# An encoder step on one Trainium2 core: half of an up projection's feature chunks by Strassen's seven products

## The chip, the core and the metric

The kernel runs on one core of one Trainium2 chip. TensorE (PE) multiplies; its weight loads (PEld) overlap with it. VectorE (DVE), ScalarE (ACT) and GpSimd (POOL) work element by element; SyncE (SP) issues DMAs. The metric is device time in microseconds, the median of several runs. A profiled execution is one run more, taken with the hardware profiler. "hi" and "lo" below are the two parts into which every float32 operand is split; TensorE multiplies in its float32r form, and a product of two operands takes three matmuls: hi x hi, hi x lo and lo x hi.

## The reference, cut to what matters

384 tokens (256 of a prompt, 16 new ones of each of 8 streams) go through one layer. The part that the change touches is the feed-forward block:

```python
h2 = rmsnorm(x, norm_ffn_g)                 # 384 x 2048
up = h2 @ w_up                              # 2048 x 11264
g_half = up[..., :D_FF]                     # D_FF = 5632
u_half = up[..., D_FF:]
ext_f = jnp.concatenate([ffn_buf.astype(g_half.dtype), g_half], axis=1)
gc = causal_dwconv(ext_f, ffn_dw_w, ffn_dw_b)          # 3 taps along the frames
x = x + (jax.nn.silu(gc) * u_half) @ w_down            # 5632 x 2048
new_ffn = ext_f[:, -(FFN_CONV_W - 1):]      # the last two rows of each stream go out as state
```

Ahead of it stand a combined input projection, attention, a convolution branch and an output projection, which the change leaves as they are, but for the last step of the output projection (below).

## The kernel before

**Tiling.** Tokens are three tiles of 128. Features are chunks of 128: 16 of them for the up projection. The 5632 columns of each half are 11 groups of 512; a *panel* is 512 columns. Group g has a gate panel and an up panel, then a convolution along the frames, SiLU, a product, and the activations `act{g}` of 4 chunks, hi and lo. The down projection reads the activations of several groups and adds to `y`, four panels of 512 columns.

**A matmul** takes one chunk of one token tile (128 x 128, loaded as weights) and 512 columns of one weight chunk. A weight tile `raw` has two chunks (512 KB, one DMA on SP's queue, three buffers). ScalarE casts it to `hi` (L149), VectorE subtracts to `lo` (L150), three buffers each. `gemm` asks for the split two tiles ahead (`ahead`), then does the 18 matmuls of the tile (2 chunks, 3 token tiles, 3 matmuls, L251 to L253): this is called a *step* below. An up panel has 8 steps, 144 matmuls. PSUM has 5 banks `acc` and 3 `misc`; a panel holds three.

**Order.** TensorE's order is the program's (`pe_order`). The other engines' order is set by the scheduler from priorities: splits get 150, what leaves PSUM 400, turns 100. `FFN_PLAN` does the up projections of groups 0 to 3, the down projection of 0 to 2, then 4 to 6 and 3 to 5, and so on.

**After a panel** ScalarE moves three banks to token rows `tok`, scaled by the row's norm (L1003). `turn` brings them to feature rows: VectorE transposes 32 x 32 blocks (L274), 16 DMAs on SP's queue move the blocks between partitions (L278, `uT<-tb`). For the gate, ScalarE copies into `extf` (L1012), GpSimd copies the halo frames (L1018, the old state at L1019), VectorE does 12 tap operations (L1027, L1029), ScalarE SiLU. `new_state` takes the last frames through a TensorE transpose (L1036) and two DMAs. For the up half, VectorE multiplies (L1058), ScalarE casts (L1060), VectorE subtracts (L1061).

**Ahead of the block**, after each panel of the output projection `norm_panel` transposes `y` and makes the feature chunks `xg`, hi (L960) and lo (L961); `second_norm` makes the row norms `rs2`.

Of the kernel before, what the change touches and what calls it, by code (L numbers as in the profile page):

```python
# [15 lines left out]
P = 128  # L16
DM = 2048
NT = 384
# [23 lines left out]
def hybrid_step(  # L42
# [27 lines left out]

    def acc_tile():
        return acc.tile([P, 512], F32, tag="acc", name="acc")

    def misc_tile():
        return misc.tile([P, 512], F32, tag="misc", name="misc")

# [51 lines left out]
    def stream_tile():  # L128
        return rp.tile([P, 2, 512], F32, tag="raw", bufs=3, name="raw")
# [44 lines left out]
    FFN_PLAN = [("up", g) for g in range(4)] + [("down", (0, 1, 2))]  # L174
    FFN_PLAN += [("up", g) for g in range(4, 7)] + [("down", (3, 4, 5))]
    FFN_PLAN += [("up", g) for g in range(7, 9)] + [("down", (6, 7))]
    FFN_PLAN += [("up", g) for g in range(9, 11)] + [("down", (8, 9, 10))]

# [8 lines left out]
    for what, g in FFN_PLAN:  # L187
        if what == "up":
# [17 lines left out]
    def ahead(n):  # L206
        while plan and len(ready) < n:
            with tc.high_priority(offset=SPLIT_AHEAD):
                if x_left and (len(plan) - v_last) in range(3, 14, 2):
                    load_x(x_left.pop(0), 2)  # L210
                ready.append(split(*fetch(plan.pop(0))))
# [16 lines left out]
    def gemm(jobs, sides=(), wide=False):  # L228
        for js in jobs:
            js = js if isinstance(js, tuple) else (js,)  # L230
            for j in js:
                nb = 4 if j["kind"] == "A" else NTT
                j["ps"] = [(misc_tile if i == 2 and (wide or j is not js[0]) else acc_tile)() for i in range(nb)]
            for j, k in [(j, k + i) for k in range(0, js[0]["nk"], 2) for j in js for i in range(2)]:
# [19 lines left out]
                if sp:  # L254
                    with tc.high_priority(offset=EVAC_AHEAD):
                        for m in range(nb):
                            j["evac"](m, ps[m])
                    if "post" in j:
                        j["post"]()
                    if "done" in j:  # L260
                        j["done"]()
# [664 lines left out]
    def open_resid():  # L926
# [5 lines left out]
        res["xg"] = [p_xg.tile([P, 2, 4, NT], F32R, name=f"xg{g}") for g in range(4)]  # L932
        p_r, res["close_r"] = pool("resid", side="right")
# [11 lines left out]
    def wo_evac(n):  # L945
        def ev(t, ps):
            ys = cols_of(res["y"], t, n)
            tt(ys, ps[:], ys, op=ALU.add)
            jk = res["f"].tile([P, 512], F32, tag="jk", bufs=1, name="jk2")
            nc.scalar.activation(jk[:], ys, AF.Square, accum_out=res["ss2"][:, t, n:n + 1])  # L950
        return ev

    def norm_panel(n):
# [3 lines left out]
        for m in range(4):  # L957
            g = col[:, R_FFN + 4 * n + m:R_FFN + 4 * n + m + 1]
            hi, lo = xg[:, 0, m, :], xg[:, 1, m, :]
            nc.scalar.activation(hi, yT[:, m], AF.Identity, scale=g)  # L960
            stt(lo, yT[:, m], g, f(hi), op0=ALU.mult, op1=ALU.subtract)  # L961

    def wo_done(n):
        def done():
            norm_panel(n)
            if n == 3:
                second_norm()
# [12 lines left out]

    p_f, y, xg, rs2, close_f, close_r = (res[k] for k in ("f", "y", "xg", "rs2", "close_f", "close_r"))
    sfT = p_f.tile([P, 44, 32], F32, name="sfT")
    sfr = p_f.tile([P, 44, 32], F32, name="sfr")
    nc.gpsimd.memset(sfr[:], 0.0)
    for a in range(4):
        nc.sync.dma_start(sfr[32 * a:32 * a + 16],
                          state_ffn[0].rearrange("b r (c a d) -> a (b r) c d", a=4, d=32)[a])
    after(8, lambda: nc.vector.transpose(sfT[:], sfr[:]))
# [3 lines left out]
    xa = grouped(xg)  # L992
    acts = {}

    def tok_rows():
        return p_f.tile([P, NTT, 512], F32, tag="tok", bufs=1, name="tok")

    def turned():
        return p_f.tile([P, 4, 4, NTT, 32], F32, tag="uT", bufs=1, name="uT")

    def up_evac(rows):
        def ev(t, ps):
            nc.scalar.activation(rows[:, t, :], ps[:], AF.Identity, scale=rs2[:, t:t + 1])  # L1003
        return ev

    def up_g_done(g, rows, sg):
        def done():
            ft = turned()
            turn(rows, ft, p_f)
            for m in range(4):  # L1010
                for t in range(NTT):
                    nc.scalar.copy(extf[:, m, 8 * t:8 * t + 8, 2:18].rearrange("p (a h) s -> p a h s", a=4),  # L1012
                                   ft[:, :, m, t, :].rearrange("p a (h s) -> p a h s", h=2))
            lc = p_f.tile([P, 18, 4], F32, tag="lc", bufs=2, name="lc")
            gcs = [p_f.tile([P, NT], F32, tag="gc", bufs=4, name="gc") for _ in range(4)]
            for m in range(4):
                e = extf[:, m]
                nc.gpsimd.tensor_copy(e[:, 1:16, 0:2], e[:, 0:15, 16:18])  # L1018
                nc.gpsimd.tensor_copy(e[:, 16:24, 0:2], sfT[:, 4 * g + m, 0:16].rearrange("p (b r) -> p b r", r=2))  # L1019
            for w in range(3):  # L1020
                for m in range(4):
                    c = 4 * g + m
                    o = gcs[m][:].rearrange("p (a t) -> p a t", t=16)
                    v = extf[:, m, :, w:w + 16]
                    wc = fw[:, w * 44 + c:w * 44 + c + 1]
                    if w == 0:
                        ts(o, v, wc, col[:, R_FDB + c:R_FDB + c + 1], op0=ALU.mult, op1=ALU.add)  # L1027
                    else:
                        stt(o, v, wc, o, op0=ALU.mult, op1=ALU.add)  # L1029
            for m in range(4):  # L1030
                nc.scalar.activation(sg[m][:], gcs[m][:], AF.Silu)
                nc.gpsimd.tensor_copy(lc[:, :, m].rearrange("p (a r) -> p a r", r=2), extf[:, m, 15:24, 16:18])

            def new_state():
                ps = misc_tile()
                tr(ps[:72, :P], lc[:].rearrange("p a m -> p (a m)"), ident[:])  # L1036
                nf = p_f.tile([72, P], F32, tag="nf", bufs=2, name="nf")
                nc.scalar.copy(nf[:], ps[:72, :P])
                cs = slice(512 * g, 512 * (g + 1))
                nc.sync.dma_start(prompt_ffn[0, 0, :, cs].rearrange("r (m p) -> r m p", m=4), nf[0:8, :])  # L1040
                nc.sync.dma_start(sample_ffn[0, :, :, cs].rearrange("b r (m p) -> (b r) m p", m=4), nf[8:72, :])
            after(10, new_state)
        return done

    def up_u_done(g, rows, sg):
        def done():
            def natural(x):
                return x.rearrange("p (t a j) -> p t a j", t=NTT, a=4)

            ft = turned()  # L1050
            if g == 10:
                uT = ft[:].rearrange("p a m t j -> p (a m t j)").rearrange("p (m x) -> p m x", m=4)
                blocks(rows[:], by_feature(uT))
            else:
                turn(rows, ft, p_f)
            for m in range(4):
                v = natural(uT[:, m]) if g == 10 else ft[:, :, m].rearrange("p a t j -> p t a j")
                tt(v, v, natural(sg[m][:]), op=ALU.mult)  # L1058
                hi, lo = natural(acts[g][:, 0, m, :]), natural(acts[g][:, 1, m, :])
                nc.scalar.copy(hi, v)  # L1060
                tt(lo, v, f(hi), op=ALU.subtract)  # L1061
        return done

    def up_jobs(g):
        sg = [p_f.tile([P, NT], F32, tag="sg", bufs=6, name="sg") for _ in range(4)]
        acts[g] = gp.tile([P, 2, 4, NT], F32R, tag=f"G{g % 4}", name=f"act{g}")
        gr, ur = tok_rows(), tok_rows()
        return [job("B", 16, xa, up_evac(gr), done=up_g_done(g, gr, sg)),
                job("B", 16, xa, up_evac(ur), done=up_u_done(g, ur, sg))]

    def down_jobs(gs, last):
        tiles = [acts[g] for g in gs]

        def evac(n):
            def ev(t, ps):
                ys = y[:, t, n * 512:(n + 1) * 512]
                tt(ys, ps[:], ys, op=ALU.add)
                if last:
                    dst = [y_prompt[0, 0:P], y_prompt[0, P:2 * P], y_sample.rearrange("b t d -> (b t) d")][t]
                    nc.sync.dma_start(dst[:, n * 512:(n + 1) * 512], ys)  # L1080
            return ev

        return [job("B", 4 * len(gs), grouped(tiles), evac(n)) for n in range(4)]

    for what, g in FFN_PLAN:
        gemm(up_jobs(g) if what == "up" else down_jobs(g, g[-1] == 10), wide=True)
# [5 lines left out]
    close_misc()  # L1092
    close_acc()
# [38 lines left out]
```

## Time and profile before

| | us |
|---|---|
| median of 3 runs | 1996.84 (1996.33 to 1998.48) |
| profiled execution | 1997.35 |
| its span | 1995.5 |
| output projection, last matmuls | about 912 |
| first up matmul to the last of the down projection | 912.4 to 1991.1 |

Rows of the profile have a line number, an engine, an operation, the tile written and those read, and a count. In a list of groups the busy time and the mean duration of one in ns come next, then the idle time of the engine just before them and what ended it. In a timeline the first two numbers are the start and the duration in us. In a table of windows each engine has its busy time and its count of instructions; the last three numbers are TensorE's granted clock (1.00 is full speed), the share of the 16 DMA engines and GB/s. A matmul's end is modelled, so the distance from start to start tells its pace.

### The profile page before, as it was taken

The numbers are of one execution on the slowest core, as the hardware profiler recorded it, in microseconds if no ns is written. First come the engines' busy times: TensorE is split into PE (matmuls) and PEld (weight loads), VectorE is DVE, ScalarE is ACT, GpSimd is POOL, SyncE is SP. The second block draws the span as 40 slices with busy tenths as digits, with TensorE's granted clock in tenths as the row PEclk, the third lists the DMA queues.
The fourth block names the chain that finished last, engine by engine and source line by source line (L and its number), as shares of the span: only waits on it lengthen the run. The fifth ranks groups of instructions, "written<-read, shape, count | busy, mean of one in ns | idle before, by whom it ended". The sixth has DMA issues, their size and how long they took to land.

```text
span 1995.5 us, 24829 instructions
## 1 busy us (share of the span) xinstructions
PE 1986.3 (100%) x9383; PEld 1677.0 (84%) x9383; DVE 1158.3 (58%) x1635; ACT 771.0 (39%) x1209; POOL 88.8 (4%) x216
## 2 busy tenths in 40 slices
PE   9999999999999999999999999999999999999999
PEld 9888999888888888888888888888888888888887
DVE  4455888888755487676455453345453345534563
ACT  5535454433334433344444442244342234323421
POOL 1000011000000000000100000000000000000000
PEclk9999999999999999999999999999999999999999
DMA  6564767444443435534555554445454445445543
GB/s 192 148 183 116 220 150 162 145 135 131 131 135 118 132 122 171 161 119 137 153 153 156 148 157 135 130 140 165 139 168 132 132 139 164 144 132 152 154 158 106
DMA packets 225384, 292.54 MB, mean 147 GB/s; under 512 B 61254, under 2 KB 112857, under 8 KB 225257
## 3 DMA queue, kind: packets, MB, share of 16 engines
q1 hardware_dynamic: 224945, 290.38, 49.7%
q8 instruction: 73, 1.20, 0.3%
q0 software_dynamic: 288, 0.57, 0.2%
q14 instruction: 46, 0.38, 0.1%
q10 hardware_dynamic: 32, 0.01, 0.0%
HBM read 266.98 MB, written 7.86 MB: 138 GB/s over the span
## 4 chain that ended last, share of the span: by engine, by line
PE 97%; DVE 2%; DMA 0%; issue 0%; SPq 0%; ACT 0%; DVEq 0%; ACTq 0%
PE acc L251 20%; PE acc L253 20%; PE acc L252 20%; PE misc L253 10%; PE misc L251 10%; PE misc L252 10%; PE acc L246 2%; PE acc L247 2%; PE acc L248 2%; DVE lo L150 0%; DVE mixT L268 0%; DMA bs<-c_dr 0%; PE misc L305 0%; PE misc L642 0%; PE misc L675 0%
## 5 line engine op out<-in xcount | busy, mean ns | idle before, releaser
L150 DVE TENSOR_TENSOR lo<-raw,hi 128x1024 fp32r<-128x1024 f32 (+2 forms) x481 | 580.3, 1207 | 676.3 <-ACT hi L149 674.1
L149 ACT CAST hi<-raw 128x1024 fp32r<-128x1024 f32 (+2 forms) x481 | 496.1, 1031 | 966.5 <-PE misc L253 781.1
L251 PE MATMUL acc<-hi,xg 128*128 128x512 f32 x704 | 275.1, 391 | 0.0
L253 PE MATMUL acc<-hi,xg 128*128 128x512 f32 x704 | 274.1, 389 | 0.0
L252 PE MATMUL acc<-lo,xg 128*128 128x512 f32 x704 | 274.1, 389 | 0.0
L251 PE MATMUL acc<-hi,hT 128*128 128x512 f32 (+1 forms) x512 | 193.4, 378 | 0.0
L253 PE MATMUL acc<-hi,hT 128*128 128x512 f32 (+1 forms) x512 | 190.7, 373 | 0.1
L252 PE MATMUL acc<-lo,hT 128*128 128x512 f32 (+1 forms) x512 | 190.7, 372 | 0.0
L251 PEld LDWEIGHTS acc<-hi,xg 128*128 128x128 f32 x704 | 132.2, 188 | 28.3
L253 PEld LDWEIGHTS acc<-hi,xg 128*128 128x128 f32 x704 | 132.2, 188 | 27.4
L766 DVE SCALAR_TENSOR_TENSOR ut<-ext,cw,ut 128x384 f32<-128x384 f32 x240 | 151.7, 632 | 6.0
L252 PEld LDWEIGHTS acc<-lo,xg 128*128 128x128 f32 x704 | 132.2, 188 | 27.0
L253 PE MATMUL misc<-hi,xg 128*128 128x512 f32 x352 | 137.1, 389 | 0.0
L251 PE MATMUL misc<-hi,xg 128*128 128x512 f32 x352 | 137.0, 389 | 0.0
L251 PE MATMUL acc<-hi,act 128*128 128x512 f32 x352 | 137.0, 389 | 0.0
L253 PE MATMUL acc<-hi,act 128*128 128x512 f32 x352 | 137.0, 389 | 0.0
L252 PE MATMUL misc<-lo,xg 128*128 128x512 f32 x352 | 137.0, 389 | 0.0
L252 PE MATMUL acc<-lo,act 128*128 128x512 f32 x352 | 137.0, 389 | 0.0
L253 PEld LDWEIGHTS acc<-hi,hT 128*128 128x128 f32 x512 | 96.4, 188 | 15.6 <-DVE hT L310 0.4
L252 PEld LDWEIGHTS acc<-lo,hT 128*128 128x128 f32 x512 | 96.5, 189 | 15.0 <-DVE lo L150 0.2
L251 PEld LDWEIGHTS acc<-hi,hT 128*128 128x128 f32 x512 | 96.5, 188 | 14.9 <-issue 0.2
L246 PE MATMUL acc<-hT,hi 128*128 128x384 f32 x256 | 89.4, 349 | 0.0
(326 smaller groups left out, 3034.9 us busy)
## 6 DMA issues: line engine op xcount, KB each, us to landing
raw<-in_w_up_dram SPq DMA_DIRECT2D x176, 512.0 KB
raw<-in_w_in_dram SPq DMA_DIRECT2D x96, 512.0 KB
raw<-in_w_down_dram SPq DMA_DIRECT2D x88, 512.0 KB
raw<-in_w_in_dram SPq DMA_DIRECT2D x64, 256.0 KB
raw<-in_w_out_dram SPq DMA_DIRECT2D x32, 512.0 KB
uT<-tb SPq DMA_DIRECT2D x336, 48.0 KB
raw<-in_w_att_out_dram SPq DMA_DIRECT2D x16, 512.0 KB
raw<-in_conv_pw_out_dram SPq DMA_DIRECT2D x16, 512.0 KB
```

The source lines that it names most:

```text
L149: queued(nc.scalar.copy(hi[:, k, :o], raw[:, k, :o]), first)
L150: queued(tt(lo[:, k, :o], raw[:, k, :o], f(hi[:, k, :o]), op=ALU.subtract), first)
L246: mm(o, hi[:, kk, s], ah, start=st, stop=False)
L247: mm(o, hi[:, kk, s], al, start=False, stop=False)
L248: mm(o, lo[:, kk, s], ah, start=False, stop=sp)
L251: mm(o, ah[:, s], hi[:, kk, :n], start=st, stop=False)
L252: mm(o, ah[:, s], lo[:, kk, :n], start=False, stop=False)
L253: mm(o, al[:, s], hi[:, kk, :n], start=False, stop=sp)
L766: stt(o, v, wc, o, op0=ALU.mult, op1=ALU.add)
```

## The change

**Seven products for eight.** Take a pair of feature chunks c0, c1 and the token tiles 0 and 1: a 2 x 2 block of x. With the pair's weights of the gate and of the up panel, another 2 x 2 block, eight block products are wanted. Strassen's scheme (in Winograd's form) takes seven, of sums of the x blocks and sums of the weight blocks. Token tile 2 has the four products that it had; two of them are taken with a sum as well, since the up panel's chunk c0 is not there by itself. A pair then has 11 products for 12, each of three matmuls. Groups 1 to 9 do this for chunks 0 to 7, four pairs; chunks 8 to 15 stay ordinary, except that they are accumulated into the seven products' banks (all eight banks of PSUM are in use). Groups 0 and 10 stay ordinary. The sums of x are made once (`sums`, `diff`) in `norm_panel`; the sums of weights are four subtractions of 128 x 512 in a pair on VectorE (`combine`), in place, per group.

**Steps.** A group has 22 steps in place of 16: "s" and "b" (12 matmuls), "c" (18, two steps), "t" (9 and 6). The chunks of "s" and "b" are loaded again for "t": 22 weight tiles in place of 16.

```diff
+    FFN_PLAN = [("up", 0)]
+    for g in range(1, 11):
+        FFN_PLAN += [("up", g), ("down", (g - 1,))]
+    FFN_PLAN += [("down", (10,))]
+    WINO = tuple(range(1, 10))
+    WINO_STEPS = [("s", 0), ("s", 1), ("b", 0), ("s", 2), ("s", 3), ("b", 2), ("c", 8), ("t", 0), ("c", 10), ("t", 1),
+                  ("c", 12), ("t", 2), ("c", 14), ("t", 3)]
...
+            if kind == "s":
+                steps.append([[(tok(2 * i, 0), 1), (tok(2 * i, 2), "g")], [(tok(2 * i + 1, 0), 2), (tok(2 * i + 1, 2), "g")]])
+            elif kind == "b":
+                steps.append([[(summed(3, kp), 3), (summed(4, kp), "u")] for kp in (i, i + 1)])
+            elif kind == "c":
+                steps.append([[(tok(k, 0), 2), (tok(k, 1), 4), (tok(k, 2), "g")] for k in (i, i + 1)])
+                steps.append([[(differ(k), 3), (tok(k, 1), 5), (tok(k, 2), "u")] for k in (i, i + 1)])
+            else:
+                steps.append([[(summed(2, i), 7), (tok(2 * i, 2), "u")], [(summed(1, i), 1)]])
+                steps.append([[(summed(0, i), 5)], [(tok(2 * i + 1, 1), 4)]])
...
+    def combine(e):
+        if e[0] == "U":
+            _, ru, rg = e
+            V.tensor_tensor(rg[:, 0, :], ru[:, 0, :], rg[:, 0, :], op=ALU.subtract)
+            V.tensor_tensor(ru[:, 0, :], ru[:, 0, :], ru[:, 1, :], op=ALU.subtract)
+            V.tensor_tensor(ru[:, 1, :], ru[:, 1, :], rg[:, 0, :], op=ALU.subtract)
+            now["DVE"] += 3 * SUM
+        elif e[0] == "G":
+            _, rg, ru = e
+            V.tensor_tensor(rg[:, 1, :], rg[:, 1, :], ru[:, 1, :], op=ALU.subtract)
+            now["DVE"] += SUM
```

**Down group by group.** The down projection of group g-1 follows the up projection of group g: 4 panels of 2 steps, and 12 additions to `y` for every group, 132 in all where there were 48.

**The order is written out.** From the feed-forward block on, every instruction on VectorE, ScalarE, GpSimd and SP is chained to the one before it on its engine (`InOrder`). A planner in the kernel's code sets the order: `step` puts a weight tile's cast, what has to leave PSUM (`fins`), the sums of a later tile (`combine`) and the subtraction to `lo`; `work` fills the rest of the step with tasks of `finish_up`, each with a cost and a time from which it is ready, as long as it would end by the step's end and SLACK. Weight tiles have six buffers, three of them in the space of an old tile.

```diff
+    MM, HI, LO, SUM, RAWS, MOVES, SLACK = 0.227, 1.05, 1.22, 0.7, 6, 7.5, 0.8
...
+        if nxt:
+            hi, lo = split_tiles()
+            with tc.high_priority(offset=high):
+                A.copy(hi[:], nxt[1][:])
...
+        for eng, cost, fn in fins:
...
+        h, l = ready.pop(0)
+        products(h, l)
+        if staged:
+            with tc.high_priority(offset=high):
+                combine(staged[0])
+        if nxt:
+            work("DVE", hi_done + 0.1)
...
+                V.tensor_tensor(lo[:], nxt[1][:], f(hi[:]), op=ALU.subtract)
...
+        for e in ("ACT", "DVE", "ACT"):
+            work(e, end + SLACK)
```

**Moves and states.** Of a turn's 16 moves GpSimd now issues 8 and SP 8. The new states go out in three DMAs that GpSimd issues, straight from the gate's token rows; the lc copies, the TensorE transpose and `nf` are gone.

```diff
+                    (G if q % 2 else S).dma_start(self.ft[32 * q:32 * q + 32, a].rearrange("p m t j -> p (m t j)"),
+                                                  self.tb[32 * a:32 * a + 32, q].rearrange("p m t j -> p (m t j)"))
...
+        G.dma_start(prompt_ffn[0, 0, :, cs], gr[P - 2:P, 1, :])
+        for r in range(2):
+            G.dma_start(sample_ffn[0, :, r, cs], gr[14 + r:P:16, 2, :])
...
+        move_u = joined(2, ut.moves() + last)
+        gate = gt.blocks() + gt.moves() + [[copies + [[move_u, conv + last]], ut.blocks() + move_u if both else [], out]]
```

**`norm_panel`** scales the transposed `y` in place, then makes hi and lo of the whole panel in one operation each, and the sums or differences with their own hi and lo:

```diff
-            hi, lo = xg[:, 0, m, :], xg[:, 1, m, :]
-            nc.scalar.activation(hi, yT[:, m], AF.Identity, scale=g)
-            stt(lo, yT[:, m], g, f(hi), op0=ALU.mult, op1=ALU.subtract)
+            nc.scalar.activation(yT[:, m], yT[:, m], AF.Identity, scale=col[:, R_FFN + 4 * n + m:R_FFN + 4 * n + m + 1])
+        nc.scalar.copy(xg[:, 0], yT[:])
+        tt(xg[:, 1], yT[:], f(xg[:, 0]), op=ALU.subtract)
```

**The order that comes of it.** First VectorE at the "t" steps of a group, in the changed program. `raw` and `raws` are weight tiles, in place differences where they are both written and read; `uT` and `act` belong to the group before.

```order
L1110 TENSOR_TENSOR lo<-raws,hi 128x1024
L1110 TENSOR_TENSOR uT<-uT,sg 128x768 x2
L1110 TENSOR_TENSOR lo<-raw,hi 128x1024
L1110 TENSOR_TENSOR raws<-raw,raws 128x512
L1110 TENSOR_TENSOR raw<-raw 128x512
L1110 TENSOR_TENSOR raw<-raw,raws 128x512
L1110 TENSOR_TENSOR lo<-raw,hi 128x1024
L1110 TENSOR_TENSOR raws<-raws,raw 128x512
```

The first lo is the tile of the "t" step of 6 matmuls, the second that of the "c" step behind it, split while the "t" step of 9 runs; the sums of the next "t" tile come after that lo and ahead of the next. Before, an up panel's rows on VectorE are a plain run of `lo<-raw,hi` with the turn's and the taps' rows between them.

Second, VectorE from the last down steps of a group into the next group, in the changed program: the taps `sg<-extf` of the group whose up projection came before.

```order
L1110 STREAM_TRANSPOSE tb<-ur 128x4x4x32 x3
L1110 TENSOR_TENSOR lo<-raw,hi 128x1024
L1110 TENSOR_TENSOR y<-bank,y 128x512 x3
L1110 TENSOR_TENSOR lo<-raw,hi 128x1024
L1110 TENSOR_TENSOR lo<-raws,hi 128x1024
L1110 TENSOR_SCALAR sg<-extf,fw,col 128x384 x2
L1110 TENSOR_TENSOR y<-bank,y 128x512 x3
L1110 TENSOR_TENSOR lo<-raws,hi 128x1024 x2
```

The first two taps now stand ahead of the last three additions to `y` and of the lo of the next group's third step; whatever delays them delays these.

Third, GpSimd, one group of before and one of the change:

```order
L1018 COPY extf<-extf 128x15x2
L1032 COPY lc<-extf 128x18
L1018 COPY extf<-extf 128x15x2
L1032 COPY lc<-extf 128x18
L1018 COPY extf<-extf 128x15x2
L1019 COPY extf<-sfT 128x8x2
```

```order
L1110 DMA uT<-tb 32x384 x8
L1110 DMA out_dram<-gr 2x512
L1110 DMA out_dram<-gr 8x512 x2
L1110 DMA uT<-tb 32x384 x8
L1110 COPY extf<-extf 128x4x15x2
L1110 COPY extf<-sfT 128x4x8x2
```

Small copies alone stood there; now the gate's 8 moves, the three state DMAs and the up half's 8 moves come ahead of the two halo copies for which the taps wait.

More of the change, by code (lines that the diff above doesn't have):

```diff
@@ L932, in open_resid @@
         res["xg"] = [p_xg.tile([P, 2, 4, NT], F32R, name=f"xg{g}") for g in range(4)]
+        res["sums"] = [p_xg.tile([P, 2, 5, 2, P], F32R, name=f"sums{n}") for n in range(2)]
         p_r, res["close_r"] = pool("resid", side="right")
@@ L991, in hybrid_step @@
         nc.gpsimd.memset(extf[:, m, 0, 0:2], 0.0)
-    xa = grouped(xg)
     acts = {}
[L995 to L1053, printed above, removed]
-            else:
[L1055 to L1062, printed above, removed]
@@ L1085, in hybrid_step, with issue, chain @@
-    for what, g in FFN_PLAN:
-        gemm(up_jobs(g) if what == "up" else down_jobs(g, g[-1] == 10), wide=True)
+    now = {"PE": 0.0, "DVE": 0.0, "ACT": 0.0, "POOL": 0.0, "SP": 0.0}
+    todo = {"DVE": [], "ACT": []}
+    def issue(eng, cost, fn, ready=0.0):
+        now[eng] = max(now[eng], ready) + cost
+        fn()
+        return now[eng]
+    def chain(ready, items):
+        if not items:
+            return
+        first, rest = items[0], items[1:]
+        if isinstance(first, list):
+            for branch in first:
+                chain(ready, branch)
+            return chain(ready, rest)
+        eng, cost, lag, fn = first
+        if eng in todo:
+            todo[eng].append((ready, cost, lag, fn, rest))
+        else:
+            chain(issue(eng, cost, fn, ready) + lag, rest)
@@ new lines, in work, with raw_tile, load @@
+    def work(eng, until):
+        while True:
+            for n, (ready, cost, lag, fn, rest) in enumerate(todo[eng]):
+                if max(ready, now[eng]) + cost <= until:
+                    break
+            else:
+                return
+            todo[eng].pop(n)
+            end = issue(eng, cost, fn, ready)
+            chain(end + lag, rest)
+    staged, pending = [], []
+    room = [RAWS]
+    def raw_tile():
+        room[0] -= 1
+        return stream_tile()
+    def load(dst, srcs):
+        for x in srcs:
+            (nc.sync if now["PE"] < 20 else S).dma_start(dst[:, :, :], x)
@@ new lines, in turn_states @@
+    def turn_states():
+        w = row_tile("ur")[:].rearrange("p t n -> p (t n)")[:, 0:44 * 32].rearrange("p (c i) -> p c i", i=32)
+        V.transpose(w, res["sfr"])
+        G.tensor_copy(sfT[:], w[:, :, 0:16])
+    chain(20.0, [("DVE", 1.7, 0.0, turn_states)])
+    for what, g in FFN_PLAN:
+        if what == "down":
+            down(g)
+        elif g in WINO:
+            wino(g)
+        else:
+            plain_up(g)
+    for _, _, fn in fins:
+        fn()
+    assert not plan and not ready and not any(todo.values())
```

370 lines of the change are left out of this document (335 added, 35 removed).

## The prediction

> **What bounds the kernel now.** I read the busy shares first, then the chain of waits, then the stretch in which the changed code runs (the feed-forward part), in that order. First the shares and the chain:
>
> ```profile
> PE 1986.3 (100%) x9383; PEld 1677.0 (84%) x9383; DVE 1158.3 (58%) x1635; ACT 771.0 (39%) x1209; POOL 88.8 (4%) x216
> PE 97%; DVE 2%; DMA 0%; issue 0%; SPq 0%; ACT 0%; DVEq 0%; ACTq 0%
> ```
>
> TensorE carries 97% of the chain that ended last. Its busy time is modelled, so I count instead. The next fence has the busy times of the feed-forward stretch, then the first and last of 28 matmuls that follow each other in one panel.
>
> ```profile
> 912.40:1991.10 1078.70, 1078.70 (x4764) 892.44 (x4763) 523.27 (x638) 392.87 (x572) 43.57 (x128) 1.00 0.48 145
> ...
> 999.66 0.39 PE L251 MATMUL misc<-hi,xg 128*128 128x512 f32 x1
> ...
> 1005.78 0.39 PE L251 MATMUL misc<-hi,xg 128*128 128x512 f32 x1
> ```
>
> 27 intervals fill 6.12 us: 0.2267 us per matmul. The stretch holds 3168 matmuls of the up projection and 1584 of the down projection (11 groups of 288 and of 144). 4752 x 0.2267 = 1077.3 of 1078.7 us, at a granted clock of 1.00. So TensorE never waits here: a matmul less is 0.227 us less, if the others still get their operands in time. VectorE (column three) is busy 523 of 1079 us, so about half of it is free.
>
> **What is removed.** A group takes 276 instead of 288 matmuls (four chunk pairs, each 11 products for 12, three matmuls each). Nine groups: 108 x 0.2267 = **24.5 us**. The order of the two programs has 119 matmuls fewer: these 108 and the 11 transposes of the new states, which now leave by DMA straight from the rows. Of a transpose the trace shows
>
> ```profile
> 965.26 0.40 PE L253 MATMUL misc<-hi,xg 128*128 128x512 f32 x1
> 965.50 0.27 PE L1036 MATMUL misc<-ident,lc 128*72 128x128 f32 x1
> 965.52 0.48 PE L251 MATMUL acc<-hi,xg 128*128 128x512 f32 x1
> 965.84 0.39 PE L252 MATMUL acc<-lo,xg 128*128 128x512 f32 x1
> ```
>
> 0.58 us for what takes two intervals (0.45) without it: 0.13 x 11 = **1.4 us**. [...]
>
> **What is added, engine by engine.** A group with its down projection now lasts (276 + 144) x 0.2267 = 95.2 us at TensorE's pace. The durations of VectorE and ScalarE, from the stretch 1010 to 1174 and the additions to y:
>
> ```profile
> L150 DVE TENSOR_TENSOR lo<-raw,hi 128x1024 fp32r<-128x1024 f32 x40 | 48.9, 1224 | 62.8 <-ACT hi L149 62.7
> L1029 DVE SCALAR_TENSOR_TENSOR gc<-extf,fw,gc 128x384 f32<-128x384 f32 x24 | 13.5, 614 | 0.1
> L274 DVE STREAM_TRANSPOSE tb<-tok 128x512 f32<-128x512 f32 x16 | 11.1, 712 | 6.7 <-ACT tok L1003 6.7
> L1027 DVE TENSOR_SCALAR gc<-extf,fw,col 128x384 f32<-128x384 f32 x12 | 5.8, 480 | 10.7 <-POOL extf L1018 10.4
> L1061 DVE TENSOR_TENSOR act<-uT,act 128x384 fp32r<-128x384 f32 x8 | 4.1, 551 | 0.0
> ...
> L1077 DVE TENSOR_TENSOR y<-acc,y x32: 675/691/693, 1197.5 to 1990.6; 128x512 f32<-128x512 f32 x32
> ...
> L149 ACT CAST hi<-raw 128x1024 fp32r<-128x1024 f32 x40 | 41.9, 1047 | 70.5 <-PE misc L253 53.6 <-DMA raw<-in_w_up_dram 12.6 <-issue 3.6
> L1003 ACT ACTIVATE tok<-acc,rs 128x512 f32<-128x512 f32 x12 | 8.2, 688 | 9.9 <-PE acc L253 9.9
> ```
>
> VectorE: 30 lo halves (22 up, 8 down) 36.7; 16 weight differences of 512 elements, by the line between 384 (0.55) and 1024 elements (1.22) 0.68 each, 10.9; 6 additions out of PSUM 4.1; 6 transposes 4.3; 12 taps 6.8; the last products and their lo halves 3.8; 12 additions to y 8.3. Sum 74.9 of 95.2 us, 79%. It has room, but it works in a fixed order, and each operation that waits holds the lo behind it. ScalarE: 30 casts 31.4 and some 9 of other work, 42%. The loads: 30 tiles of 0.52 MB and 1.6 MB of moves, 17.3 MB in 95.2 us, 182 GB/s. The stretch above moved 145 GB/s at a share of 0.48, so 182 is about 0.6 of the 16 engines; they are no bound, and six raw buffers cover twice the lead of three.
>
> **Where it could wait.** Three places, each with its spare time. First, the short steps. How a weight tile is split around a step's first matmul (1002.38):
>
> ```profile
> 1002.38 0.39 PE L251 MATMUL acc<-hi,xg 128*128 128x512 f32 x1
> ...
> 1002.62 1.05 ACT L149 CAST hi<-raw 128x1024 fp32r<-128x1024 f32 x1 [2.70 <-PE misc L253]
> ...
> 1003.70 1.23 DVE L150 TENSOR_TENSOR lo<-raw,hi 128x1024 fp32r<-128x1024 f32 x1 [2.07 <-ACT hi L149]
> ```
>
> Done 2.55 us after the step began; it is wanted two steps on, by the second matmul. Before, that is 36 matmuls or 8.16 us away. The two "t" steps have 9 and 6 matmuls: 3.40 + 0.23 = 3.63 us, spare 1.1. The code's planner may let another operation run 0.8 us (its SLACK) over the boundary on either engine, which this spare just covers; an addition out of PSUM on top (0.69) would make 0.4 us of stall, four times a group. Bounds: 0 to 1.6 us a group, 0 to 14 in nine; below 0 is excluded, since nothing here shortens a matmul. I take 0.3 a group, **2.7 us**, near the low end: the order has no such addition ahead of that lo.
>
> Second, at the end of a group three sums leave PSUM through ScalarE and then VectorE ahead of the lo of the second down step. With 0.69 for each: done 6.7 us after the last t pair began, wanted at 3.40 + 4.08 + 0.23 = 7.7. Spare 1.0, taken as nothing.
>
> Third, the convolution. The taps stand in VectorE's order ahead of additions to y and of a lo for the next group's third step, and wait for GpSimd's halo copies, which stand behind 8 moves that GpSimd now issues itself. Nearest rows (GpSimd's and SP's issues, landing, and first use after 16 moves):
>
> ```profile
> 4.25 0.50 POOL L369 DMA_DIRECT2D vrow<-in_q_norm_g_dram  x1
> 4.75 0.57 POOL L371 DMA_DIRECT2D kg<-in_k_norm_g_dram  x1
> ...
> DMA to landing us min/median/max: 2.4/3.0/4.8
> ...
> L278 SPq DMA_DIRECT2D uT<-tb x336: 507/589/1687, 946.8 to 1871.5; - x168
> ...
> 1012.20 10.25 SPq L278 DMA_DIRECT2D uT<-tb  x16
> ...
> 1023.95 1.70 ACT L1012 COPY extf<-uT 128x128 f32<-128x128 f32 x8 [4.01 <-DMA uT<-tb]
> ```
>
> From the start of the down steps: gate rows transposed at 9.9; 8 issues of 0.54 on GpSimd to 14.2; landed 17.2; ScalarE's four copies (0.5 each) sit behind the casts of the fifth and sixth step and end at 22.2; 8 more issues to 26.5; halo at 27.2. The taps come up at 31.1 at the earliest, behind the eighth step's lo. The halo may come as late as 34.0 (the lo behind it is wanted at 32.65 + 24 x 0.2267 + 0.23 = 38.3, and 0.96 of taps, 2.07 of additions and 1.22 of itself lie before). Spare 6.8 us: nothing.
>
> Once only, the last feature panel's halves take a longer way (scaled in place, then copied, some 4 us more on ScalarE and VectorE):
>
> ```profile
> L961 DVE SCALAR_TENSOR_TENSOR xg<-yT,col,xg x16: 608/612/619, 829.1 to 930.2; 128x384 fp32r<-128x384 f32 x16
> ```
>
> Ready at 930.8, then about 935; wanted 108 matmuls after 912.4, at 936.9. Nothing. The end is as before: three additions and their stores.
>
> **Sum.** The profiled execution took 1997.35 us (span 1995.5): 1997.35 - 24.5 - 1.4 + 2.7 = 1974.2. The median is 0.5 below that execution: **1974 us**.
>
> **Rivals.** (1) *GpSimd's issues are slow, and the kernel gets slower.* For: it issues hardly any DMA in the part shown, its rows are from the idle start, and one of SP's moves took 1.69 us. Against: eight in a row at 0.50 to 0.68 there. It counts twice, in the gate's moves and the up rows' moves. At 1.0 us an issue the halo comes at 32.7, still in time; at 1.25 at 36.7, 2.7 late, times nine 24 us: no gain; at 1.4 at 39.1, 5.1 late, 46 us: 2020. So it costs from 1.1 us an issue on and makes the kernel slower from 1.3 on. [...]
>
> (2) *VectorE's spare is gone.* 79% busy in a fixed order; if each t pair loses the 0.4 us above, 14 us: 1986; if it loses 0.7 (one more addition's length) there is no gain, 1997. For: a spare of 1.1 us where there were 5.6. Against: the order puts the long work into the long steps.
>
> (3) *Fewer matmuls, same time*, because they would run at a wider pitch: 4644 x 0.005 = 23 us. Their shapes and their alternation of banks are as before; nothing speaks for it. The count itself is in the order.
>
> **How the numbers follow.** Forecast 0.65 (1970 to 1981), VectorE 0.18 (1981 to 1997), GpSimd 0.14, of which 0.02 stop at no gain, pitch 0.03. A measurement of this kernel tells 0.2%, 4 us, from no change. Faster: 0.65 + 0.15 of VectorE = 0.80; within 4 us: 0.03 + 0.02 + 0.02 = 0.07; slower 0.13. The range runs from 1969.5 (no stall at all, 1997.35 - 25.9 - 0.5 = 1970.9, less some of the 2 us by which the runs before differ) to 1992, through most of VectorE's case; GpSimd's case is left out.
>
> **What would show it.** Right: 4644 matmuls and no transposes between the first up matmul and the last down one, at 0.2267, the stretch near 1055 us; lo ends before its step; GpSimd's moves near 0.54 us; idle TensorE a few us. Wrong: VectorE idle until GpSimd's extf with TensorE idle until lo right after (rival 1), TensorE idle until lo in the t steps (rival 2), or a pitch above 0.227 (rival 3).

## The result and the profile after

| | before | after |
|---|---|---|
| median, us | 1997.42 (1996.33 to 1998.48, 4 runs) | 1972.19 (1971.93 to 1972.51, 4 runs) |
| profiled execution, us | 1997.35 | 1972.51 |
| its span, us | 1995.5 | 1970.8 |
| first up matmul starts | 912.45 | 913.41 |
| last matmul of the down projection starts | 1990.88 | 1965.83 |

The changed kernel is faster: ratio 0.9874, 95% interval 0.9857 to 0.9891. The busy shares and the chain of waits on its page:

```profile
PE 1960.6 (99%) x9264; PEld 1655.2 (84%) x9264; DVE 1389.2 (70%) x1918; ACT 808.2 (41%) x1119; POOL 160.0 (8%) x320
...
PE 97%; DVE 2%; DMA 1%; SPq 0%; issue 0%; ACT 0%; DVEq 0%; ACTq 0%
```

TensorE still bounds it, with 119 matmuls fewer; VectorE went from 1158 to 1389 us and GpSimd from 89 to 160. Where the time went is read from the feed-forward stretch. Its row in the table of windows (PE, PEld, DVE, ACT, POOL, granted clock, share of the DMA engines, GB/s):

```profile
912.40:1967.50 1055.10, 1053.82 (x4650) 872.26 (x4648) 752.95 (x920) 423.63 (x477) 114.26 (x232) 1.00 0.56 175
```

The first and the last matmul in the timeline:

```profile
913.41 0.39 PE L1352 MATMUL bank<-hi,xg 128*128 128x512 f32 x1
...
1965.83 0.39 PE L1354 MATMUL bank<-hi,act 128*128 128x512 f32 x1
```

Between the two starts lie 1052.42 us; 4644 matmuls have 4643 intervals, and 4643 x 0.22667 = 1052.4. Nothing is left over: TensorE did not wait once between them, and the view of TensorE's waits from 890 to 1975 has no row. Before, the same two starts were 1078.43 us apart. The stretch gave 26.0 us; it started 1.0 us later. That is no effect of the change: the same start lies between 911.5 and 913.6 in the runs below, and at 912.6 when the changed kernel ran again.

The first spare time of the prediction, at a "t" pair that began at about 1384.0, and the second, at the end of a group, in the timeline of VectorE and TensorE:

```profile
1385.30 1.23 DVE L1110 TENSOR_TENSOR lo<-raw,hi 128x1024 fp32r<-128x1024 f32 x1 [0.77 <-ACT hi L1110]
...
1387.60 0.39 PE L1353 MATMUL bank<-lo,xg 128*128 128x512 f32 x1
...
1423.89 1.22 DVE L1110 TENSOR_TENSOR lo<-raw,hi 128x1024 fp32r<-128x1024 f32 x1
...
1426.36 0.39 PE L1353 MATMUL bank<-lo,act 128*128 128x512 f32 x1
```

The first lo ends at 1386.53 and is read from 1387.60 on: 1.1 us to spare, as at nearly all 36 "t" pairs (the least is 0.8). The second ends at 1425.11 and is read at 1426.36: 1.25 us. The third, the halo of a group whose down steps start at 1422.05, in the timeline of TensorE, GpSimd and VectorE:

```profile
1422.05 0.39 PE L1352 MATMUL bank<-hi,act 128*128 128x512 f32 x1
...
1431.84 3.92 POOL L1110 DMA_DIRECT2D uT<-tb  x8 [77.30 <-DMA raw<-in_w_up_dram]
1435.75 1.62 POOL L1110 DMA_DIRECT2D out_dram<-gr  x3
1444.41 3.98 POOL L1110 DMA_DIRECT2D uT<-tb  x8 [7.04 <-ACT extf L1110]
1447.82 1.23 DVE L1110 TENSOR_TENSOR lo<-raw,hi 128x1024 fp32r<-128x1024 f32 x1 [0.40 <-ACT hi L1110]
1448.38 0.82 POOL L1110 COPY extf<-extf 128x120 f32<-128x120 f32 x1
1449.14 0.23 POOL L1110 COPY extf<-sfT 128x64 f32<-128x64 f32 x1
...
1453.04 0.86 DVE L1110 TENSOR_SCALAR sg<-extf,fw,col 128x384 f32<-128x384 f32 x2
```

Eight issues take 3.92 us. The halo is there 27.3 us after the start of the down steps (27.7 in every second group), and the taps come up at 31.0, not waiting for it.

### The profile page after: what moved, and what is told of

Same layout as the page of the kernel before. It is cut to its first block, busy times and chain, and to the rows that moved or that the text cites. A ratio compares the mean times of both kernels' runs of the same rounds, so it can differ in the third digit from the quotient of the medians.

```text
span 1970.8 us, 25327 instructions
## 1 busy us (share of the span) xinstructions
PE 1960.6 (99%) x9264; PEld 1655.2 (84%) x9264; DVE 1389.2 (70%) x1918; ACT 808.2 (41%) x1119; POOL 160.0 (8%) x320
## 4 chain that ended last, share of the span: by engine, by line
PE 97%; DVE 2%; DMA 1%; SPq 0%; issue 0%; ACT 0%; DVEq 0%; ACTq 0%
PE bank L1354 18%; PE bank L1352 18%; PE bank L1353 18%; PE acc L311 8%; PE acc L313 8%; PE acc L312 8%; PE misc L312 4%; PE misc L313 4%; PE misc L311 4%; PE acc L306 2%; PE acc L307 2%; PE acc L308 2%; DVE lo L168 0%; DVE mixT L330 0%; DMA raw<-in_w_in_dram 0%; DMA bs<-c_dr 0%
## 5 line engine op out<-in xcount | busy, mean ns | idle before, releaser
L168 DVE TENSOR_TENSOR lo<-raw,hi 128x1024 fp32r<-128x1024 f32 (+2 forms) x219 | 259.3, 1184 | 199.9 <-ACT hi L167 198.1
L167 ACT CAST hi<-raw 128x1024 fp32r<-128x1024 f32 (+2 forms) x219 | 221.7, 1012 | 398.3 <-PE misc L313 308.5
L1110 ACT CAST hi<-raws 128x1024 fp32r<-128x1024 f32 x157 | 165.6, 1055 | 333.0 <-PE bank L1354 315.0
L1352 PE MATMUL bank<-hi,xg 128*128 128x512 f32 x768 | 298.8, 389 | 0.0
L1353 PE MATMUL bank<-lo,xg 128*128 128x512 f32 x768 | 298.8, 389 | 0.0
L1354 PE MATMUL bank<-hi,xg 128*128 128x512 f32 x768 | 298.8, 389 | 0.0
L1110 DVE TENSOR_TENSOR lo<-raw,hi 128x1024 fp32r<-128x1024 f32 x159 | 194.5, 1223 | 131.9 <-ACT hi L1110 131.9
L1110 DVE TENSOR_TENSOR lo<-raws,hi 128x1024 fp32r<-128x1024 f32 x157 | 191.9, 1222 | 135.5 <-ACT hi L1110 135.5
L1110 ACT CAST hi<-raw 128x1024 fp32r<-128x1024 f32 x159 | 166.8, 1049 | 278.1 <-PE bank L1354 200.2
L1352 PE MATMUL bank<-hi,act 128*128 128x512 f32 x528 | 205.4, 389 | 0.0
L1353 PE MATMUL bank<-lo,act 128*128 128x512 f32 x528 | 205.4, 389 | 0.0
L1354 PE MATMUL bank<-hi,act 128*128 128x512 f32 x528 | 205.4, 389 | 0.0
L1354 PEld LDWEIGHTS bank<-hi,xg 128*128 128x128 f32 x768 | 144.1, 188 | 30.0
L1352 PEld LDWEIGHTS bank<-hi,xg 128*128 128x128 f32 x768 | 144.1, 188 | 29.9
```

The costliest lines, as they stand in the source:

```text
L167: queued(nc.scalar.copy(hi[:, k, :o], raw[:, k, :o]), first)
L168: queued(tt(lo[:, k, :o], raw[:, k, :o], f(hi[:, k, :o]), op=ALU.subtract), first)
L1110: d = op(*args, **kw)
L1352: mm(o, ah, h[:, kk, :], start=start, stop=False, **kw)
L1353: mm(o, ah, l[:, kk, :], start=False, stop=False, **kw)
L1354: mm(o, al, h[:, kk, :], start=False, stop=stop, **kw)
```

## Experiments

Each difference is against the changed kernel. It ran a second time, together with experiment 3 and the 20 issues of experiment 4, at 1970.58 us (1970.00 to 1971.73, ratio 0.9867, interval 0.9853 to 0.9882). So the median of one and the same kernel moved by 1.6 us from one set of runs to another, to a little below what was expected:

> The changed kernel as it is, beside the two that follow: 1972.2 us, 1971 to 1973.

**1. All groups ordinary.**

```diff
-    WINO = tuple(range(1, 10))
+    WINO = ()
```

> All eleven groups take ordinary products (288 matmuls each); the changed order of work, the down projection group by group, the moves shared with GpSimd, the new banks and the state rows by DMA stay. Theory (the gain is 108 matmuls at 0.2267 us each and hardly anything else): 1972.2 + 24.5 = 1996.7 us, that is 0 to 1.5 below the kernel before. Rival (the order, the banks and the down projection group by group brought part of the gain): 1972 to 1990, each us below 1996 being theirs.

Measured: 1996.30 us, ratio to before 0.9993 (0.9985 to 1.0002). The stretch:

```profile
911.50:1990.00 1078.50, 1077.32 (x4753) 891.71 (x4752) 563.78 (x667) 373.37 (x432) 111.78 (x232) 1.00 0.49 145
```

The new order, the banks, the moves by GpSimd and the down projection group by group are worth nothing that can be measured by themselves: the gain is the 108 matmuls. From the first to the last matmul this kernel takes 1076.9 us, 1.5 less than before (the transposes of the states, 1.4 in the sum) and 24.5 more than the changed kernel.

**2. The first spare time, used up from one side.** In each step of nine matmuls VectorE does k additions that nobody reads, between hi and lo:

```diff
+            if mults == 9:
+                spare = p_f.tile([P, 512], mybir.dt.bfloat16, tag="spare", bufs=1, name="spare")
+                for _ in range(k):
+                    V.tensor_tensor(spare[:], f(hi[:, 0, :]), f(hi[:, 1, :]), op=ALU.add)
             with tc.high_priority(offset=high):
                 V.tensor_tensor(lo[:], nxt[1][:], f(hi[:]), op=ALU.subtract)
```

One addition:

> In each of the 36 steps with nine matmuls VectorE does one useless addition of 128x512 (some 0.69 us) that reads the hi half just before the lo of the same tile, so that this lo ends 0.69 later. Theory (that lo has 1.1 us to spare): 0 to 1 us more than the changed kernel, 1972 to 1973. Rival (the spare is used up already, so that each delay counts): 36 x 0.69 = 25 us more, 1997.

Three additions:

> The same with three useless additions, 2.07 us, ahead of the lo of each nine-matmul step. Theory (spare 1.1 us): each of the 36 steps loses 2.07 - 1.1 = 0.97 us, 35 us in all, about 2007 (1998 to 2017), with TensorE idle until lo at the start of the tenth to eighteenth matmul after that step's begin. Rival A (the wait is not at this lo; other buffers give more lead): 1972 to 1975. Rival B (no spare): 36 x 2.07 = 75 us, 2047.

Measured: 1971.38 us with one (ratio 0.9872, 0.9858 to 0.9885), no wait; 2014.41 with three (1.0086, 1.0073 to 1.0100). With three, VectorE's group of additions:

```profile
L1110 DVE TENSOR_TENSOR spare<-hi 128x512 bf16<-128x512 f32 x108 | 74.8, 692 | 76.1 <-ACT hi L1110 73.7
```

TensorE's waits in the stretch (us in total, times, the longest), then its timeline around one of them:

```profile
PE bank L1357 <- DVE lo L1110: 31.7, 36, 1.2
```

```profile
1405.99 0.39 PE L1356 MATMUL bank<-hi,xg 128*128 128x512 f32 x1
1407.25 0.50 PE L1357 MATMUL bank<-lo,xg 128*128 128x512 f32 x1 [0.87 <-DVE lo L1110]
1407.59 0.40 PE L1358 MATMUL bank<-hi,xg 128*128 128x512 f32 x1
1407.83 0.40 PE L1356 MATMUL bank<-hi,xg 128*128 128x512 f32 x1
```

36 waits, one for each "t" pair, at the matmul that the prediction named. A start comes 1.26 us after the one before it, 1.03 late, where 2.07 - 1.1 = 0.97 was forecast; the next starts come at 0.34 and 0.24 in place of 0.227. Counted over the twelve intervals from the start before it on, this wait costs 1.21 us and the 36 cost 1.19 on average: 42.8 in all, which is what the stretch is longer in this trace (1095.2 us against 1052.4; the medians differ by 42.2). The whole loss lies at this place, while VectorE's share of the span only goes from 70% to 72%: the spare time decides, not the share.

**3. The second spare time.** Three such additions only in the last short step of a group (`ending` is true when `j == len(steps) - 1`).

```diff
+            if ending[0]:
+                ...
+                for _ in range(3):
+                    V.tensor_tensor(spare[:], f(hi[:, 0, :]), f(hi[:, 1, :]), op=ALU.add)
```

> Three useless additions of 128x512, 2.07 us, ahead of the lo of the last short step of each of the nine groups, the one that already waits for three sums out of PSUM. In the changed kernel's trace this lo ends at 1425.1 and is wanted at 1426.4. Theory (spare 1.0 to 1.3 us): 0.8 to 1.1 us late in nine groups, and 0.3 more for each wait as in the run with three additions in 36 steps (42 us where 31.7 were waited): 10 to 13 us more, 1982 to 1985, TensorE waiting nine times for lo. Rival A (the sums move behind and the lo is not later): 1972. Rival B (the later sums out of PSUM hold the banks and the transposes too, and the loss grows): above 1995.

Measured: 1980.07 us (ratio 0.9915, 0.9900 to 0.9929), 9.5 above the changed kernel beside it. TensorE's waits:

```profile
PE bank L1358 <- DVE lo L1110: 6.2, 9, 0.7
```

VectorE and TensorE in the timeline at one of them:

```profile
1426.99 2.13 DVE L1110 TENSOR_TENSOR spare<-hi 128x512 bf16<-128x512 f32 x3
1429.04 1.22 DVE L1110 TENSOR_TENSOR lo<-raw,hi 128x1024 fp32r<-128x1024 f32 x1
...
1430.31 0.50 PE L1358 MATMUL bank<-lo,act 128*128 128x512 f32 x1 [0.69 <-DVE lo L1110]
```

Nine waits of 0.69, each costing 1.0 us in starts: 9.0, a little less than the 10 to 13 that were expected of this run. With 2.07 us more the matmul that reads this lo starts 0.85 late, so the spare was 1.2, as read from the trace after; the prediction had 1.0.

**4. GpSimd's queue (rival 1).** GpSimd issues all 16 moves of a turn; then 4 or 8 useless small ones ahead of them.

```diff
-                    (G if q % 2 else S).dma_start(self.ft[32 * q:32 * q + 32, a].rearrange("p m t j -> p (m t j)"),
+                    G.dma_start(self.ft[32 * q:32 * q + 32, a].rearrange("p m t j -> p (m t j)"),
```

The useless moves (two for each a with 24 issues, one with 20):

```diff
+            more = p_f.tile([P, 2, 96], F32, tag="more", bufs=1, name="more")
+            for a in range(4):
+                for q in range(2):
+                    G.dma_start(more[32 * a:32 * a + 32, q], self.tb[32 * a:32 * a + 32, q].rearrange("p m t j -> p (m t j)")[:, 0:96])
```

> GpSimd issues all 16 moves of a turn, SP none: as if its issues took 1.0 instead of 0.5 us. The gate's moves land some 3.9 us later and the up rows' moves end some 7.8 us later, so that the halo comes at 27.3 + 3.9 to 7.8 us = 31 to 35 after the start of the down steps, with 34.0 the latest that costs nothing. Theory: 0 to 10 us more than the changed kernel, 1972 to 1982. Rival (GpSimd's queue is on the path already): 3.9 to 7.8 us for each of 10 groups, 2011 to 2050.

> The same, and eight more small useless moves (32 rows of 768 bytes into a tile that nobody reads) ahead of each turn's 16, all issued by GpSimd: 24 issues of 0.5 us a turn where there were 8. Halo at 27.3 + 2 x 16 x 0.5 = 43 at the most, 35 at the least. Theory (34.0 is the latest that costs nothing, beyond it each us late is a us lost in each of 10 groups): 10 to 90 us more, 1982 to 2062, and TensorE idle until the lo that stands behind the taps. Rival (the taps' wait is covered further by other work): 1972 to 1976.

> Four useless moves ahead of each turn's 16, all by GpSimd. With none of them the halo came 33.1 us after the start of the down steps and TensorE did not wait; with eight it came at 41.0 and TensorE waited 6.4 us. Theory (each issue counts 0.5 us twice a group): halo near 37, TensorE waits some 2.5 to 3 us, 9 or 10 times, 22 to 30 us in all. What the clock does after such a wait: if it stays at 1.00 as after waits of 1 us, 1997 to 2006 us; if it falls to 0.50 for some 3 us as after 6.4 us, 1.8 us more each time, 2013 to 2024. Rival (the wait does not grow with the issues but with the landing of the additional moves): 1974 or above 2040.

| issues by GpSimd in a turn | median, us | ratio to before | waits of TensorE |
|---|---|---|---|
| 8 (changed kernel) | 1970.58 | 0.9867 (0.9853 to 0.9882) | none |
| 16 | 1973.77 | 0.9884 (0.9869 to 0.9898) | none listed; one start 0.21 us late |
| 20 | 2020.54 | 1.0114 (1.0098 to 1.0131) | 35.1 us in 9 |
| 24 | 2052.62 | 1.0275 (1.0260 to 1.0291) | 59.7 us in 10 |

With 16: the start of a group's down steps, its halo and the taps, in the timeline of TensorE, GpSimd and VectorE:

```profile
1327.34 0.39 PE L1352 MATMUL bank<-hi,act 128*128 128x512 f32 x1
...
1359.97 0.31 POOL L1110 COPY extf<-extf 128x120 f32<-128x120 f32 x1
1360.20 0.25 POOL L1110 COPY extf<-sfT 128x64 f32<-128x64 f32 x1
...
1360.49 0.87 DVE L1110 TENSOR_SCALAR sg<-extf,fw,col 128x384 f32<-128x384 f32 x2 [2.07 <-POOL extf L1110]
```

The halo comes at 33.1; VectorE stands idle for it for 2.07 us, and TensorE does not notice. In the nine groups it comes at 32.7 to 34.6, and only behind the one at 34.6 a start of TensorE is 0.21 us late; the interval of the time overlaps with that of the changed kernel. With 24, the same places of the timeline and TensorE's wait:

```profile
1356.97 0.39 PE L1356 MATMUL bank<-hi,act 128*128 128x512 f32 x1
...
1397.71 0.25 POOL L1110 COPY extf<-sfT 128x64 f32<-128x64 f32 x1
1397.99 0.87 DVE L1110 TENSOR_SCALAR sg<-extf,fw,col 128x384 f32<-128x384 f32 x2 [9.70 <-POOL extf L1110]
...
1401.84 0.80 PE L1357 MATMUL bank<-lo,sums 128*128 128x512 f32 x1 [6.40 <-DVE lo L1110]
1402.43 0.63 PE L1358 MATMUL bank<-hi,sums 128*128 128x512 f32 x1
```

The halo comes at 41.0 and the matmul that reads the lo behind it is 6.6 us late in its start (6.79 after the one before it, in place of 0.23): so 34.4 is the latest that costs nothing, where the prediction had 34.0. The one late start with 16 issues gives 34.4 as well. The price of being later is more than the wait, though: at 20 issues 50.0 us were lost and 35.1 waited; the last section tells why. The median with 20 lies inside the 2013 to 2024 that were expected of it, but not by the steps that gave this range. They had halos near 37, waits of 2.5 to 3 us and 1.8 us more for each; the halos came at 37.5 to 40.5, the waits were 1.9 to 5.9, and each cost 0.3 to 3.2 more than its length. One reason that the trace shows is that GpSimd's issues stand idle here and there until earlier moves have landed (2.1 us in the second turn of the group whose down steps start at 1345.74).

**5. Fewer raw tiles.** `RAWS` from 6 to 3: the planner keeps three weight tiles in flight.

> The order is made for three raw tiles in flight instead of six (a step's loads start later). Theory (the loads are no bound but the short steps use four tiles in 6.8 us, so a lead of three tiles is short there): some tiles arrive late, 5 to 30 us more, 1977 to 2002, TensorE idle until lo with DMA as what ended its wait's cause. Rival (a load lands within its step and six buffers are not needed): 1972 to 1974.

Measured: 1974.78 us (ratio 0.9889, 0.9872 to 0.9905), with two waits of TensorE in the stretch:

```profile
PE bank L1353 <- DVE lo L1110: 1.9, 2, 1.1
```

The theory of this run, that three tiles are too few at the short steps, held in one group, at a price below its range, and fell in the other eight. Both waits, at 1000.1 and 1008.7, are in group 1, the first by seven products, where VectorE's sums come late because of a load:

```profile
996.77 2.15 DVE L1110 TENSOR_TENSOR raws<-raws 128x512 f32<-128x512 f32 x3 [5.17 <-DMA raws<-in_w_up_dram]
```

The two waits, each 0.3 us dearer than its row as in experiment 2, make 2.5 us, and the stretch is 2.5 longer. In this trace that is what the lead of six is worth.

**6. A looser planner.** `SLACK` from 0.8 to 2.5 us.

> The planner lets other work on ScalarE and VectorE run 2.5 us over a step's end instead of 0.8, so that additions and taps stand ahead of more lo halves. Theory (the short steps have 1.1 us to spare, and 0.8 was just covered): stalls of up to 1.4 us in some of the 36 short pairs, 5 to 40 us more, 1977 to 2012. Rival (the planner's times are looser than the chip's, and the order does not decide): 1972 to 1974.

Measured: 1971.35 us (ratio 0.9871, 0.9856 to 0.9885), no wait of TensorE. This theory fell as well. The order on VectorE does differ (taps and transposes stand one lo earlier in several places), but, as far as the order was read, no addition out of PSUM moves ahead of a lo of a "t" pair, and the spare at the 36 pairs is 1.1 us in this trace too.

**7. One more pair by seven products.** Five chunk pairs in place of four, the steps of 18 matmuls laid between any two "t" pairs, and a step "e" of six matmuls for the fifth pair's share of "b".

```diff
-    WINO_STEPS = [("s", 0), ("s", 1), ("b", 0), ("s", 2), ("s", 3), ("b", 2), ("c", 8), ("t", 0), ("c", 10), ("t", 1),
-                  ("c", 12), ("t", 2), ("c", 14), ("t", 3)]
+    WINO_STEPS = [("s", 0), ("s", 1), ("b", 0), ("s", 2), ("e", 8), ("s", 3), ("b", 2), ("s", 4), ("g", 10), ("t", 0),
+                  ("u", 10), ("t", 1), ("g", 12), ("t", 2), ("u", 12), ("t", 3), ("g", 14), ("u", 14), ("t", 4)]
...
+            elif kind == "e":
+                steps.append([[], [(summed(3, i // 2), 3), (summed(4, i // 2), "u")]])
```

> Five instead of four chunk pairs of groups 1 to 9 by seven products, with the steps in another order (a gate or an up step of 18 matmuls between any two pairs of short steps): 3 matmuls less in each group, 27 x 0.2267 = 6.1 us, for four more weight differences and 1.5 more lo halves a group (4.6 us of VectorE, 80 of 94.5 us). Theory (TensorE's count sets the time while VectorE keeps its order in time): 1966.1 us (1965 to 1968). Rival (the tighter order stalls; 0.5 us for each of five short pairs, 22 us): 1975 to 1990.

Measured: 1966.81 us (1965.22 to 1967.27), ratio 0.9848 (0.9834 to 0.9861): the fastest of all. The stretch:

```profile
912.00:1961.00 1049.00, 1047.33 (x4619) 866.40 (x4617) 798.24 (x974) 443.71 (x496) 114.22 (x232) 1.00 0.61 185
```

TensorE's only wait in it:

```profile
PE bank L1361 <- DVE lo L1118: 0.9, 1, 0.9
```

From the first to the last matmul 1047.6 us, 4.8 less than the changed kernel: 6.1 for 27 matmuls, and 1.2 given back in one wait with its restart. The wait, at 1006.7, is again in group 1, behind a load that came late; from then on no wait of VectorE is listed until that lo is done:

```profile
994.73 0.69 DVE L1118 TENSOR_TENSOR raw<-raws,raw 128x512 f32<-128x512 f32 x1 [2.46 <-DMA raw<-in_w_up_dram]
```

VectorE is busy 798 of 1049 us, 76%. That the steps' new arrangement was needed for this was not tried.

## Why the prediction was right, point by point

**The bound and the count** held. The stretch was forecast near 1055 us with 4644 matmuls at 0.2267 and has just that. The first term, 24.5, is what experiment 1 gives back in the trace (24.5); in the medians it is 1996.3 - 1972.2 = 24.1. The second, 1.4 for the transposes, measured 1.5.

**The third term was mis-sized: 2.7 us for stalls, measured 0.** It stood for "an addition out of PSUM on top" ahead of a lo in a "t" pair, and the prediction itself saw that the order has none. The spare time at that place, 1.1 us, was exact: experiment 2 puts its edge between 0.69 and 2.07 and finds a start 1.03 late at 2.07. But what the planner may place there was priced as a chance, when the order could be read for it: with no such operation in the order, the term is 0. 1997.35 - 24.5 - 1.5 = 1971.3; the profiled execution took 1972.5, since the stretch started 1.0 later and what follows its last matmul took 0.3 longer. That the forecast of 1974 lies only 1.8 above the median is in part luck: the later start, which the sum did not have, hides some of the 2.7.

**The second spare time** was 1.0 forecast, 1.25 in the trace and 1.2 by experiment 3. Taking it as nothing was right.

**The third** followed its steps closely: halo forecast at 27.2 and seen at 27.3 or 27.7, taps at 31.1 and 31.0, latest halo 34.0 and by experiment 4 34.4. The steps leave out the three state DMAs, 1.62 us of GpSimd; they fall into its wait for ScalarE's copies (7.04 us in the group shown) and cost nothing. The price of an issue, 0.50 to 0.57 us from GpSimd's rows at the start of the program, held in the busy part (groups of GpSimd in the stretch: busy time, mean ns of one, idle time before it):

```profile
L1110 POOL DMA_DIRECT2D uT<-tb x176 | 87.0, 502 | 845.4 <-DMA raw<-in_w_up_dram 722.1 <-DVE tb L1110 97.7 <-ACT extf L1110 21.1
L1110 POOL COPY extf<-extf 128x120 f32<-128x120 f32 x11 | 5.9, 536 | 11.2 <-ACT extf L1110 11.2
```

**Rival 1 (GpSimd's issues)** was a real mechanism at a price that did not come. Its points were right where the runs reach them. 16 issues of 0.5 us stand for 8 of 1.0, "still in time", and they are. Its 2020 us stood for a halo at 39.1, 5.1 us late, and 46 us lost. With 20 issues the halo came at 38.8 on average, TensorE's starts were 4.1 us late and the stretch lost 51.5. That the median is 2020.5 is a coincidence: a us of lateness costs more than the us that the rival counted, and there were fewer of them. Where the halo meets a lo of VectorE it is later, but not by much: in the group shown above the halo's first copy starts 0.56 us into a lo of 1.23 and takes 0.82 us. Five of the eleven first copies do so; the other six start when the lo before them has ended and take 0.29 to 0.31, and those in the run with 24 issues, for which VectorE waits, 0.30. It lost 0.5 us, somewhat less than the 0.67 that were left of that lo, and the second copy (0.23), which starts after that lo, nothing.

**Rival 2 (VectorE's spare)** needed 0.4 us lost in each "t" pair and saw none; experiment 2 shows what it would have looked like. VectorE's share was as forecast: its rows in the group from 1326.85 to 1422.05 add up to 75.1 us, where 74.9 were estimated. **Rival 3 (a wider pitch)** is excluded by 4643 intervals at 0.22667.

**The loads and the last panel**, both taken as nothing: in that same group 183 GB/s at a share of 0.58, where 182 and 0.6 were estimated, and half the lead would do but for 2.5 us in group 1 (experiment 5). The last panel's halves were ready at 935.7 in the trace after, with the matmul that wants them at 937.9.

## What to carry to other kernels

Where one engine runs back to back and nothing else is on its path, count its instructions times their spacing, and then look for the tightest places: for each, the time at which an operand is done and the time at which it is read. The differences, not the busy shares, tell what can be added: VectorE at 71% and at 76% cost next to nothing, while 2.1 us more ahead of one lo in each of 36 "t" pairs cost 42 us, and 0.7 us there nothing. Where the order is fixed, read from it whether an operation can come in at such a place, and put no term into the sum for one that does not stand there.

## What the hardware showed unasked

**The longer waits of TensorE cost its clock as well: one of 3.39 us did, one of 2.93 us did not.** Both are in the run with 20 issues; the start after each wait and the two that follow, in the timeline:

```profile
1487.72 0.50 PE L1356 MATMUL bank<-lo,sums 128*128 128x512 f32 x1 [2.93 <-DVE lo L1110]
1488.06 0.39 PE L1357 MATMUL bank<-hi,sums 128*128 128x512 f32 x1
1488.29 0.40 PE L1355 MATMUL bank<-hi,sums 128*128 128x512 f32 x1
...
1285.82 0.80 PE L1356 MATMUL bank<-lo,sums 128*128 128x512 f32 x1 [3.39 <-DVE lo L1110]
1286.41 0.63 PE L1357 MATMUL bank<-hi,sums 128*128 128x512 f32 x1
1286.84 0.63 PE L1355 MATMUL bank<-hi,sums 128*128 128x512 f32 x1
```

The table of windows around them (the granted clock is the third number from the right):

```profile
1486.00:1488.00 2.00, 0.28 (x1) 0.28 (x2) 2.00 (x3) 0.00 (x0) 0.00 (x0) 1.00 0.00 0
1488.00:1490.00 2.00, 2.00 (x10) 1.62 (x10) 2.00 (x4) 0.00 (x0) 0.00 (x0) 1.00 0.60 129
...
1284.00:1286.00 2.00, 0.18 (x1) 0.18 (x2) 2.00 (x4) 0.00 (x0) 0.00 (x0) 0.79 0.00 0
1286.00:1288.00 2.00, 2.00 (x5) 1.62 (x6) 2.00 (x4) 0.00 (x0) 0.00 (x0) 0.50 0.52 115
1288.00:1290.00 2.00, 2.00 (x6) 1.52 (x6) 1.88 (x3) 0.00 (x0) 0.00 (x0) 0.50 0.92 306
```

After 2.93 us of idleness the clock stays at 1.00 and the matmuls go on at 0.23. After 3.39 us it has fallen to 0.50 and they come at 0.43 for 6.1 us more, until 1291.96. Counted from the start before a wait until the starts come at 0.227 again, the wait of 2.93 costs 3.2 us and that of 3.39 costs 6.6. Of the nine waits of this run the two under 3 us cost 0.3 more than their length and the seven over 3.3 us 1.8 to 3.2 more; all nine add up to 51.5, by which this trace's stretch is longer than the changed kernel's (1103.9 us against 1052.4; the medians differ by 50.0). The extra does not grow with the length of the wait (3.2 for 3.39 us, 1.8 for 5.93), and the clock need not fall during it: after the wait of 3.81 us the next starts come at 0.34, 0.24, 0.23 and 0.24, and the first matmul that is longer again (0.51 for 0.40) stands 1.3 us behind the wait. By the tables of windows and the starts the clock is at 0.50 for about 6.8 us around the wait of 3.39 us and for about 3.4 around that of 3.58. The prediction's prices for a late halo lacked this. What decides whether the clock falls after a wait, and for how long, the runs do not show.

**A short wait costs 0.3 us more than it shows** (1.21 us of starts for a row of 0.87 in experiment 2, 1.0 for 0.69 in experiment 3): the matmul behind it is longer (0.50 for 0.39), the next start comes at 0.34 and those after it a little wide (0.23 to 0.24 for 0.227), at a clock of 1.00. What makes them wide was not looked into.
